# The down projections of a two-FFN block: 16 turns of at most three pairs in place of 14 of at most four, with another order of the seven products

## The chip, the cores and the metric

The kernel runs on one core of a Trainium2 chip. The metric is device microseconds of one execution. The profile is of one execution of its own, with its own time; the other times are of runs without a profile.

## The reference

One layer over a sequence of 1024 positions and 1024 features, in float32: x = x + ½·SwiGLU₁(norm(x)); then a mixer (eight heads of stick-breaking attention beside a gated short convolution) that adds to x; then x = x + ½·SwiGLU₂(norm(x)); a last norm. What matters here are the two FFNs:

```
def swiglu(h, w_gate, w_up, w_down):
    return (jax.nn.silu(h @ w_gate) * (h @ w_up)) @ w_down
```

w_gate and w_up are 1024 × 2816, w_down is 2816 × 1024. The change touches the two products with w_down, called the down phases.

## The kernel before, in words

**Arithmetic.** Every float32 operand of a matmul is split in two parts, a rounded one (`hi`, written by ACT, line 169) and the rest (`lo`, written by DVE, line 170), and three matmuls make one product (`mm3`, line 221). On top of that the FFNs use a 2 × 2 block scheme with seven products in place of eight, P1, P2, P3, P5, P6, P7 and Q4. Each product has a left factor (the stationary operand) and a right factor (the moving one), which are sums and differences of the four blocks. Two products can share a PSUM bank (`BANK`, line 562): P1 and P2 have bank 0, P6 bank 1, P7 and Q4 bank 2, P5 and P3 bank 3. The first of two that share has to be taken out of PSUM before the second may be added on top of it.

**A down phase.** The 2816 hidden features are 22 tiles of 128, or 11 pairs; `NQ` is 11. The output is cut into four groups g; a group is the output tiles g and g + 4, in two halves of 512. So there are 44 units (a pair for a group), each of seven products of three matmuls of 128 × 128 by 128 × 512, or 21 matmuls. A **turn** (`Turn`, line 782) runs one group over some consecutive pairs q0 to q1, product by product. `UPTO` and `TURNS` (lines 374 and 375) list the turns: here 14, over 2, 3, 4, 4, 3, 3, 3, 4, 4, 4, 4, 3, 2 and 1 pairs. The first ten end before the last pair: ACT and DVE take their products out of PSUM (lines 802 to 829), and each sends four accumulating DMAs, which add 256 KB to memory each (line 795, issued by POOL: 40 in a phase). The last four turns, one per group, add into tiles that were read back (`back`) and call `ready` four times (lines 831 to 855). In the first down phase `ready` is `to_mixer` (line 963: split with the gain, squares for the next norm, a store); in the second it is `to_output` (line 1326: squares, the final norm, the store of the result).

**Factors.** The left factors of a turn are made during the turn before it, one step after each product. In the first phase they come from w_down (`left`, line 463; raw tiles in two buffers, loaded by `L.load`), in the second from memory (`left_back`, line 500, which loads seven factors and splits them). The right factors of a pair are made once and kept in SBUF until the last turn that needs them: in the first phase from memory (`right_back`, line 723, which has one load under way ahead of the split), in the second from w_down (`right_rows`, line 738). `down_prep` (line 770) steps the left and the right generators of a turn side by side. The seven products run in the order `FEW`: P1, P6, P2, P7, P5, Q4, P3.

**Buffers.** Tiles of 128 × 512 (`s`, line 58) have 72 buffers, those of 128 × 1024 (`w4`, line 62) ten. The left factors of one turn take six of the ten (three pairs of hi and lo; the seventh factor is in `s` tiles), and raw or intermediate tiles take more.

**Order.** The framework puts the instructions of each engine in one queue, nearly in the order in which the program states them, and each engine runs its queue in order; matmuls of neighbouring products may be mixed. All plain loads are on SP's queue in order, all accumulating DMAs on POOL's. An instruction that waits for a buffer or for data holds up all behind it on its engine.

After the first down phase comes the V projection (line 981), which takes the features in the order of `VORDER` (line 435): tiles 2 and 6, then 3 and 7, 0 and 4, 1 and 5. After the second one nothing follows but the stores.

## Time and profile before

| | us |
|---|---|
| median of three runs | 1953.84 (1951.84 to 1957.67) |
| the profiled execution: its time | 1946.61 |
| the profiled execution: its span | 1944.9 |
| mean granted clock of TensorE, of full speed | 0.977 |

A row of windows gives a stretch: its length, then the busy time of each engine with its number of instructions, the granted clock of TensorE, the share of the 16 DMA engines and GB/s. A row of waits tells who waited for whom: microseconds in total, times, the longest. A row of groups has the shape, the number of instructions, busy time and the mean ns of one, then the idle time of the engine before them. PE is TensorE, DVE is VectorE, ACT is ScalarE, POOL is GpSimd, SP is SyncE.

### The profile page before, as it was taken

The numbers are of one execution on the slowest core, as the hardware profiler recorded it, in microseconds if no ns is written. First come the engines' busy times: TensorE is split into PE (matmuls) and PEld (weight loads), VectorE is DVE, ScalarE is ACT, GpSimd is POOL, SyncE is SP. The second block draws the span as 40 slices with busy tenths as digits, with TensorE's granted clock in tenths as the row PEclk, the third lists the DMA queues.
The fourth block names the chain that finished last, engine by engine and source line by source line (L and its number), as shares of the span: only waits on it lengthen the run. The fifth ranks groups of instructions, "written<-read, shape, count | busy, mean of one in ns | idle before, by whom it ended". The sixth has DMA issues, their size and how long they took to land. (4 is left out here: it accounts for less than half of the span.)

```text
span 1944.9 us, 23049 instructions
## 1 busy us (share of the span) xinstructions
PE 1845.2 (95%) x8176; PEld 1506.7 (77%) x8176; DVE 1384.8 (71%) x2145; ACT 887.6 (46%) x1576; POOL 238.2 (12%) x384
## 2 busy tenths in 40 slices
PE   6889999999898989999999999989999999889996
PEld 5668888888677768888888877867888888667784
DVE  4897666666766698577787898668666666657667
ACT  4543222233544446567687785533322222345443
POOL 1101101000121111110101000200101001012111
PEclk8899999999999999999999999999999999989998
DMA  7114333324787843432313333313333333488864
GB/s 233 65 55 135 106 104 111 103 93 143 203 214 194 220 154 101 95 77 60 96 37 78 97 107 117 129 38 103 114 109 104 108 101 109 147 209 190 214 166 153
DMA packets 250277, 242.73 MB, mean 125 GB/s; under 512 B 13568, under 2 KB 196400, under 8 KB 250160
## 3 DMA queue, kind: packets, MB, share of 16 engines
q1 hardware_dynamic: 216720, 157.87, 26.8%
q0 software_dynamic: 33440, 83.38, 16.6%
q8 instruction: 64, 1.05, 0.2%
q14 instruction: 53, 0.43, 0.1%
HBM read 150.76 MB, written 81.00 MB: 119 GB/s over the span
## 5 line engine op out<-in xcount | busy, mean ns | idle before, releaser
L91 PE MATMUL ps<-s,w 128*128 128x512 f32 x6352 | 1533.2, 395 | 72.0 <-ACT s L169 19.7
L91 PEld LDWEIGHTS ps<-s,w 128*128 128x128 f32 x6352 | 1192.6, 190 | 339.4 <-ACT s L169 24.5
L169 ACT CAST w<-raw 128x1024 fp32r<-128x1024 f32 (+3 forms) x154 | 156.9, 1019 | 271.5 <-PE ps L91 167.8
L170 DVE TENSOR_TENSOR w<-raw,w 128x1024 fp32r<-128x1024 f32 (+3 forms) x154 | 181.6, 1180 | 110.9 <-PE ps L91 61.3
L91 PE MATMUL ps<-s,s 128*128 128x512 f32 (+3 forms) x968 | 246.6, 382 | 14.0 <-DVE s L835 8.5
L91 PEld LDWEIGHTS ps<-s,s 128*128 128x128 f32 x968 | 181.7, 189 | 55.9 <-ACT s L818 6.7
L634 POOL DMA_DIRECT2D c_sp<-s x154 | 83.5, 542 | 782.4 <-DVE s L620 618.7
L170 DVE TENSOR_TENSOR w<-w,w 128x1024 fp32r<-128x1024 f32 (+3 forms) x96 | 104.6, 1090 | 95.4 <-PE ps L91 48.6
L170 DVE TENSOR_TENSOR s<-s,s 128x512 fp32r<-128x512 f32 (+2 forms) x190 | 125.7, 676 | 58.0 <-ACT s L169 56.9
L169 ACT CAST s<-s 128x512 fp32r<-128x512 f32 (+2 forms) x190 | 111.4, 611 | 73.5 <-DMA s<-c_sp 45.9
L169 ACT CAST w<-w 128x1024 fp32r<-128x1024 f32 (+3 forms) x96 | 90.1, 938 | 98.4 <-DMA w<-c_sp 86.6
L616 ACT ACTIVATE s<-s 128x512 f32<-128x512 f32 x40 | 25.3, 633 | 209.1 <-DVE s L615 209.1
L484 DVE TENSOR_TENSOR w<-raw 128x1024 f32<-128x1024 f32 (+3 forms) x54 | 62.9, 1164 | 56.0 <-PE ps L91 55.9
L170 DVE TENSOR_TENSOR s<-raw,s 128x512 fp32r<-128x512 f32 (+2 forms) x120 | 78.5, 672 | 13.0 <-ACT s L169 12.7
L601 ACT ACTIVATE s<-ps 128x512 f32<-128x512 f32 x40 | 23.8, 598 | 122.8 <-PE ps L91 122.8
L169 ACT CAST s<-raw 128x512 fp32r<-128x512 f32 (+2 forms) x120 | 70.7, 607 | 8.1 <-DMA raw<-in_ffn_w_down 8.1
L1204 DVE TENSOR_TENSOR s<-s,ps 128x128 f32<-128x128 f32 (+2 forms) x96 | 52.7, 549 | 16.8 <-ACT s L1200 16.4
L1192 ACT ACTIVATE s<-ps 128x128 f32<-128x128 f32 (+2 forms) x96 | 47.0, 490 | 37.7 <-PE ps L91 37.3
L607 DVE TENSOR_TENSOR s<-s,ps 128x512 f32<-128x512 f32 x40 | 27.4, 686 | 47.8 <-PE ps L91 47.8
L1200 ACT ACTIVATE s<-s 128x128 f32<-128x128 f32 (+2 forms) x96 | 50.2, 523 | 20.9 <-DVE s L1196 19.7
L637 DVE TENSOR_TENSOR s<-s,s 128x512 f32<-128x512 f32 x88 | 56.8, 687 | 1.3
L620 DVE SCALAR_TENSOR_TENSOR s<-s,s 128x512 f32<-128x512 f32 x80 | 54.8, 687 | 1.9 <-ACT s L616 0.7
(135 smaller groups left out, 1639.1 us busy)
## 6 DMA issues: line engine op xcount, KB each, us to landing
c_sp<-s POOLq DMA_DIRECT2D x154, 256.0 KB, 2.5
raw<-in_ffn_w_gate SPq DMA_DIRECT2D x43, 512.0 KB, 3.9
raw<-in_ffn_w_up SPq DMA_DIRECT2D x43, 512.0 KB, 5.2
s<-c_sp SPq DMA_DIRECT2D x83, 256.0 KB, 6.4
x_sp<-s POOLq DMA_DIRECT2D x72, 256.0 KB, 4.1
r_sp<-s POOLq DMA_DIRECT2D x56, 256.0 KB, 4.5
raw<-in_ffn_w_down SPq DMA_DIRECT2D x11, 1024.0 KB, 7.7
raw<-in_w_in SPq DMA_DIRECT2D x20, 512.0 KB, 3.8
```

The lines of the kernel that those rows point to most:

```text
L91: nc.tensor.matmul(out, lhs, rhs, **kw)
L169: nc.scalar.copy(hi, x)
L170: nc.vector.tensor_tensor(out=lo, in0=x, in1=f(hi), op=ALU.subtract)
L484: nc.vector.tensor_tensor(out=two(y), in0=two(blk(1, 2)), in1=blk(3).unsqueeze(1).to_broadcast([P, 2, n]), op=ALU.add)
L607: nc.vector.tensor_tensor(out=self.u3, in0=self.u2, in1=self.o[2], op=ALU.add)
L616: last_silu[0] = nc.scalar.activation(self.u2, self.u2, AF.Silu)
L620: nc.vector.scalar_tensor_tensor(out=u, in0=u, scalar=-0.5, in1=g, op0=ALU.mult, op1=ALU.mult)
L634: nc.gpsimd.dma_start(out=self.sp[FACTORS.index(self.names[i]), j], in_=x)
L637: nc.vector.tensor_tensor(out=out, in0=x, in1=y, op=op)
L1192: behind(nc.scalar.activation(u["s"][:, cols], u["z"][:, cols], AF.Exp), table_set)
L1200: nc.scalar.activation(sc, sc, AF.Ln, bias=1.0)
L1204: nc.vector.tensor_tensor(out=sc, in0=sc, in1=u["z"][:, cols], op=ALU.max)
```

## The change

The turns get other lengths: 16 turns over 2, then twelve of 3, then 2, 2 and 2 pairs (the thirteenth, the first of the last four, has 3). Their products run in a new order, P1, P7, P5, P6, P2, Q4, P3. The right factors are no longer tied to a turn: a list `MADE` says how many of the 77 are made by the end of each turn, and they are made one after the other. In the first phase four loads are under way ahead of the split. The left factors are made in the order P2/P1, P7/P5, P3/P6, Q4; in the second phase each load of them stands one step ahead of its split. In the last turns of the groups the order of the additions differs. The gate and up part keeps its order. `VORDER` stays.

```diff
@@ -371,12 +371,9 @@
     c_sp = [dr.tile([7, NQ, P, HALF], F32, name=f"c_sp{i}") for i in range(2)]
 
 
-    UPTO = (2, 3, 4, 4, 5, 6, 7, 8, 9, 10) + (NQ,) * 4
+    UPTO = (2, 3, 3, 3, 5, 6, 6, 6, 8, 9, 9, 9) + (NQ,) * 4
+    MADE = (21, 22, 25, 35, 42, 43, 46, 56, 63, 64, 67) + (7 * NQ,) * 5
     TURNS = [(i % 4, UPTO[i - 4] if i > 3 else 0, n) for i, n in enumerate(UPTO)]
-
-    def news(i):
-
-        return range(UPTO[i - 1] if i else 0, UPTO[i])
 
     def part(c0, src, **kw):
 
@@ -393,14 +390,14 @@
             yield [part(j * S, w[:, m * P : (m + 1) * P]) for j, w in enumerate((wg, wu))]
         for j, (g, q0, q1) in enumerate(TURNS):
             if i:
-                for q in news(j):
-                    yield [part(0, wd[2 * q * P : 2 * (q + 1) * P])]
                 continue
             n = (q1 - q0) * P
             rows = wd[2 * q0 * P : 2 * q1 * P].rearrange("(k two p) c -> two p k c", two=2, p=P)
             yield [(b * n, n, (lambda a: a.rearrange("p (k c) -> p k c", c=P)),
                     rows[two, :, :, d * P : (d + 1) * P])
                    for b, (two, d) in enumerate(((1, g), (0, g), (1, g + 4), (0, g + 4)))]
+        for q in range(NQ * i):
+            yield [part(0, wd[2 * q * P : 2 * (q + 1) * P])]
 
     def mixer_weights():
         def columns(c0):
@@ -460,7 +457,8 @@
 
 
 
-    def left(raw, n=HALF):
+    def left(raw, n=HALF, late="P7"):
+
 
         a = {}
 
@@ -486,13 +484,18 @@
         nc.vector.tensor_tensor(out=blk(3), in0=y[:, :n], in1=blk(2), op=ALU.add)
         nc.vector.tensor_tensor(out=blk(0), in0=blk(3), in1=blk(0), op=ALU.add)
         yield
-        z = two(raw[:, : 4 * n])[:, 0::3]
-        hi, lo = pair(), pair()
-        split(two(hi), two(lo), z)
-        halves(hi, lo, "P3", "P6")
-        yield
-        halves(*split(pair(), pair(), y), "P7", "P5")
-        yield
+
+        def wide():
+            hi, lo = pair(), pair()
+            split(two(hi), two(lo), two(raw[:, : 4 * n])[:, 0::3])
+            halves(hi, lo, "P3", "P6")
+
+        def narrow():
+            halves(*split(pair(), pair(), y), "P7", "P5")
+
+        for step in (wide, narrow) if late == "P7" else (narrow, wide):
+            step()
+            yield
         a["Q4"] = split(s(F32R)[:, :n], s(F32R)[:, :n], blk(2))
         L.load()
         yield
@@ -506,17 +509,26 @@
             nc.sync.dma_start(out=to.rearrange("p (k c) -> p k c", c=P),
                               in_=c_sp[1][i, q0:q1, :, g * P : (g + 1) * P].rearrange("k p c -> p k c"))
 
-        yield a
-        for i in (0, 2, 4):
+        def begin(i):
             raw = w4(F32)[:, : 2 * n]
             for j in range(2):
                 load(raw[:, j * n : (j + 1) * n], i + j)
-            parts = split(w4()[:, : 2 * n], w4()[:, : 2 * n], raw)
+            return raw
+
+        yield a
+        raw = begin(0)
+        yield
+        for i, after_it in ((0, 4), (4, 2), (2, 6)):
+            now = raw
+            if after_it < 6:
+                raw = begin(after_it)
+            else:
+                raw = s()[:, :n]
+                load(raw, 6)
+            parts = split(w4()[:, : 2 * n], w4()[:, : 2 * n], now)
             for j in range(2):
                 a[FACTORS[i + j]] = tuple(x[:, j * n : (j + 1) * n] for x in parts)
             yield
-        raw = s()[:, :n]
-        load(raw, 6)
         a["Q4"] = split(s(F32R)[:, :n], s(F32R)[:, :n], raw)
         yield
 
@@ -712,72 +724,95 @@
                 prep = left(L.take()[0])
                 a = next(prep)
             else:
-                prep = down_prep(i, 0)
-            for name in FEW:
+                prep = iter(())
+                makers[i] = Prep(i)
+                makers[i].begin(0)
+            for n, name in enumerate(FEW):
                 unit.do(name)
                 next(prep, None)
+                if i in makers:
+                    makers[i].step()
+                    makers[i].upto(UPTO[0] * (n + 1))
             run(prep)
+        makers[i].end()
 
     ring, lefts = {}, {}
 
-    def right_back(q):
-
-        b = ring[q] = {}
-
-        def load(name):
-            raw = s()
-            nc.sync.dma_start(out=raw, in_=c_sp[0][FACTORS.index(name), q])
-            return raw
-
-        raw = load(FEW[0])
-        for i, name in enumerate(FEW):
-            now, raw = raw, load(FEW[i + 1]) if i < 6 else None
-            b[name] = split(s(F32R), s(F32R), now)
+    ORDER = ("P1", "P7", "P5", "P6", "P2", "Q4", "P3")
+
+    def rights_back(ahead=4):
+
+        todo = [(q, name) for q in range(NQ) for name in ORDER]
+        raws = []
+
+        def load():
+            q, name = todo[len(raws)]
+            raws.append(s())
+            nc.sync.dma_start(out=raws[-1], in_=c_sp[0][FACTORS.index(name), q])
+
+        for i, (q, name) in enumerate(todo):
+            while len(raws) < min(len(todo), i + ahead):
+                load()
+            ring.setdefault(q, {})[name] = split(s(F32R), s(F32R), raws[i])
             yield
 
-    def right_rows(q):
-
-        b = ring[q] = {}
-        raw, _ = L.take()
-        b11, b12, b21, b22 = (raw[:, i * HALF : (i + 1) * HALF] for i in range(4))
+    def rights_rows():
+
+
+        def done(name, x):
+            b[name] = split(s(F32R), s(F32R), x)
 
         def comb(out, x, y, op):
             nc.vector.tensor_tensor(out=out, in0=x, in1=y, op=op)
             return out
 
-        def done(name, x):
-            b[name] = split(s(F32R), s(F32R), x)
-
...
+        for q in range(NQ):
+            b = ring[q] = {}
+            raw, _ = L.take()
+            b11, b12, b21, b22 = (raw[:, i * HALF : (i + 1) * HALF] for i in range(4))
+            done("P1", b11)
+            comb(b11, b11, b12, ALU.subtract)
             yield
+            done("P7", comb(b12, b22, b12, ALU.subtract))
+            yield
+            done("P5", b11)
+            yield
+            done("P6", comb(b11, b11, b22, ALU.add))
+            yield
+            done("P2", b21)
+            comb(b21, b11, b21, ALU.subtract)
+            yield
+            done("Q4", b21)
+            yield
+            done("P3", b22)
+            L.load()
+            yield
+
+    class Prep:
+
+
+        def __init__(self, i):
+            self.i, self.made, self.lefts = i, 0, iter(())
+            self.rights = rights_rows() if i else rights_back()
+
+        def upto(self, n):
+            while self.made < n:
+                next(self.rights)
+                self.made += 1
+
+        def begin(self, j):
+            if j < len(TURNS):
+                g, q0, q1 = TURNS[j]
+                self.lefts = left_back(g, q0, q1) if self.i else left(L.take()[0], (q1 - q0) * P, "P3")
+                lefts[j] = next(self.lefts)
+
+        def step(self):
+            next(self.lefts, None)
+
+        def end(self):
+            run(self.lefts)
+
+    makers = {}
 
     class Turn(Blocks):
 
@@ -836,17 +871,15 @@
 
             if name == "P6":
                 u = self.kept.pop(self.g)
+                comb(x(1, 1), u, ALU.subtract)
+                ready(self.g + 4, 1)
+                comb(x(1, 0), u, ALU.subtract)
                 comb(x(0, 1), u, ALU.add)
-                comb(x(1, 1), u, ALU.subtract)
-                comb(x(1, 0), u, ALU.subtract)
             if name == "P2":
                 comb(x(0, 0), o, ALU.add)
                 ready(self.g, 0)
-            if name == "P7":
+            if name in ("P7", "P5"):
                 comb(x(1, 1), o, ALU.subtract)
-            if name == "P5":
-                comb(x(1, 1), o, ALU.subtract)
-                ready(self.g + 4, 1)
             if name == "Q4":
                 comb(x(1, 0), o, ALU.subtract)
                 ready(self.g + 4, 0)
@@ -856,17 +889,21 @@
 
     def down(i, acc, tiles, back, ready):
 
-        for j, (g, q0, q1) in enumerate(TURNS):
-            prep = down_prep(i, j + 1) if j + 1 < len(TURNS) else iter(())
-            if j + 1 >= NQ - 1 and j + 1 < len(TURNS):
+        prep = makers.pop(i)
+        for j in range(len(TURNS)):
+            k = j + 1
+            prep.begin(k)
+            if len(TURNS) - 4 <= k < len(TURNS):
                 for hf in range(2):
-                    back((j + 1) % 4, hf)
-                    back((j + 1) % 4 + 4, hf)
+                    back(k % 4, hf)
+                    back(k % 4 + 4, hf)
             turn = Turn(j, acc, tiles)
-            for name in FEW:
+            made = MADE[j - 1] if j else 7 * UPTO[0]
+            for n, name in enumerate(ORDER):
                 turn.do(name, ready)
-                next(prep, None)
-            run(prep)
+                prep.step()
+                prep.upto(made + (MADE[j] - made) * (n + 1) // 7)
+            prep.end()
         ring.clear()
         lefts.clear()
 
```

## Rows read from the trace of the kernel before

**Rows 1.** The page's first line.
```profile
span 1944.9 us, 23049 instructions
```

**Rows 2.** Windows: first down phase (two rows), V stage, second down phase (four), end.
```profile
core 0: us, PE busy (x) PEld busy (x) DVE busy (x) ACT busy (x) POOL busy (x), PEclk, DMA share, GB/s
494.00:671.00 177.00, 162.46 (x691) 129.23 (x690) 114.94 (x159) 87.53 (x146) 35.36 (x42) 0.99 0.79 200
671.00:728.00 57.00, 48.41 (x203) 38.33 (x202) 50.73 (x86) 24.38 (x41) 8.50 (x15) 0.94 0.52 165
728.00:752.00 24.00, 24.00 (x108) 19.57 (x107) 15.93 (x31) 15.29 (x33) 5.35 (x10) 0.94 0.38 131
1689.00:1876.00 187.00, 168.82 (x694) 132.60 (x693) 120.27 (x172) 90.05 (x148) 36.15 (x43) 0.95 0.85 207
1876.00:1895.00 19.00, 19.00 (x85) 15.73 (x85) 11.83 (x20) 6.02 (x12) 1.67 (x2) 1.00 0.57 151
1876.00:1936.00 60.00, 51.78 (x210) 39.93 (x209) 43.96 (x86) 20.85 (x48) 6.31 (x7) 0.94 0.51 155
1936.00:1945.00 9.00, 0.20 (x1) 0.00 (x0) 3.23 (x8) 2.57 (x6) 1.85 (x2) 0.50 0.31 117
```

**Rows 3.** Waits, 494 to 671 us: who waited for whom, total, times, longest.
```profile
ACT s L169 <- DMA s<-c_sp: 38.5, 12, 8.9
PE ps L91 <- ACT s L818: 4.6, 3, 2.6
PE ps L91 <- ACT s L169: 3.4, 1, 3.4
```

**Rows 4.** Waits, 1689 to 1876 us.
```profile
ACT w L169 <- DMA w<-c_sp: 59.1, 21, 6.2
ACT s L169 <- DMA raw<-in_ffn_w_down: 8.1, 1, 8.1
PE ps L91 <- ACT s L169: 6.5, 3, 4.1
PE ps L91 <- DVE s L820: 5.2, 5, 1.8
```

**Rows 5.** Waits of SP's queue: first phase, then second.
```profile
SPq L191 <- DVE s L170: 125.3, 13, 13.1
...
SPq L506 <- PE ps L91: 130.2, 30, 8.3
```

**Rows 6.** Windows of 5 us, columns as in rows 2.
```profile
605.00:610.00 5.00, 5.00 (x16) 3.95 (x17) 5.00 (x8) 2.68 (x6) 1.73 (x2) 0.70 0.41 57
1700.00:1705.00 5.00, 3.29 (x6) 1.57 (x6) 3.37 (x5) 1.24 (x2) 0.00 (x0) 0.52 1.05 319
1805.00:1810.00 5.00, 5.00 (x24) 4.14 (x23) 3.74 (x5) 2.45 (x6) 1.59 (x2) 1.00 1.11 328
```

**Rows 7.** DMA queues and issues: 494 to 671 us, then 1689 to 1876.
```profile
q0 software_dynamic: 5816, 11.07, 37.0%
s<-c_sp SPq DMA_DIRECT2D x57, 256.0 KB, 7.5
...
q0 software_dynamic: 5835, 11.23, 37.5%
w<-c_sp SPq DMA_DIRECT2D x36, 256.0 KB, 5.2
w<-c_sp SPq DMA_DIRECT2D x22, 192.0 KB, 3.7
```

**Rows 8.** Groups by line, 494 to 671 us: what takes products out of PSUM.
```profile
L795 POOL DMA_DIRECT2D x_sp<-s x39 | 33.8, 869 | 140.3 <-ACT s L814 77.4 <-DVE s L820 20.8 <-ACT s L828 18.0
L820 DVE TENSOR_TENSOR s<-s,ps 128x512 f32<-128x512 f32 x10 | 6.8, 680 | 0.2 <-ACT s L818 0.2
L814 ACT COPY s<-ps 128x512 f32<-128x512 f32 x10 | 5.8, 579 | 3.2 <-PE ps L91 3.2
```

**Rows 9.** Timeline of the last turn: start, us, engine, line, operation, idle before it.
```profile
1923.52 0.41 ACT L169 CAST w<-w 128x256 fp32r<-128x256 f32 x1 [5.68 <-DMA w<-c_sp]
...
1928.74 2.80 PE L91 MATMUL ps<-s,w 128*128 128x512 f32 x6 [3.34 <-ACT w L169]
...
1936.24 0.69 DVE L835 TENSOR_TENSOR s<-s,ps 128x512 f32<-128x512 f32 x1
```

27 lines of the change are left out of this document (removed).

## The prediction, made before the change was run

> **What bounds the kernel now.** I read the page's first line, then windows over both down phases, then the waits inside them, then queues and groups. The span is 1944.9 us [rows 1]; the profiled execution's own time is 1946.61, so 1.7 lie around the span. The median of the three runs is 1953.84, 0.37% higher; the sum is made against 1946.6 and carried to the median by that ratio. The change touches only the two down phases, so only their idle time is at stake.
>
> I cut each phase at its last four turns. The cut comes after 34 of the 44 units: the first phase is 177.0 us for 34 units and 57.0 for ten, the second 187.0 and 60.0, and 9.0 after the last product [rows 2]. The clean rate comes from 1876 to 1895: TensorE is busy for all of 19.00 us at full clock, and this is the turn of four pairs, 84 matmuls (the row counts 85, one being cut by the window's edge). So a matmul costs 0.227 us and a unit of 21 matmuls 4.77 us. 34 units are 162 us clean, ten are 47.7. What is lost now: 15 and 25 us in the long stretches, 9 and 12 us in the last turns. 44 units stay 44 units, so the matmuls' own time cannot change; the four losses can.
>
> Why the long stretches lose: in the first phase ACT stands 38.5 us before casts of right factors, until their loads land, 8.9 at the longest [rows 3]. ACT's queue is in order, so the copy of P7 out of PSUM (line 818), behind such a cast, comes late and TensorE waits for it, 4.6 us, and 3.4 for a cast itself [rows 3]. The loads are late because SP's queue is in order too: the next raw w_down load (line 191) waits 13 times, up to 13.1 us, for DVE to free its buffer, and the single load ahead of the right factors is behind it [rows 5]. In the second phase it is the left factors: ACT waits 59.1 us for them [rows 4], since their 30 loads wait for TensorE to give back one of the ten wide buffers, 130 us on SP's queue [rows 5]; TensorE then waits for line 820, behind them on DVE, in five turns [rows 4]. A single wait of 8.1 us for w_down [rows 4] is the start of the second phase: pair 2 is requested only when pair 0's buffer is free, and pairs 0 and 1 were made side by side. A long idle stretch also costs clock: after 603 us the granted clock is 0.70 of full, after 1700 it is 0.52 [rows 6], which is the lower level, 1.2 GHz, for most of these stretches.
>
> **The change, part by part.**
>
> *Order of the products.* Bank 0 is used again three products later instead of one (P1, then P7, P5, P6, then P2), bank 2 three instead of one, bank 3 three instead of one. With three pairs a product is 9 × 0.227 = 2.0 us, so an eviction has 6 us in place of 2 (2.7 with four pairs). A late copy behind a cast, the 4.6 us of rows 3 and the 5.2 of rows 4, is covered unless it is over 6 us late. The order also frees the wide buffers as they are needed: P7/P5 go free after the third product, P2/P1 after the fifth, and the new left factors are made in an order that fits into ten. So DVE no longer stands before a `lo` part until a product has run.
>
> *Loads ahead.* Right factors: four of the 77 under way. On average 4.8 factors are made per turn of 14.3 us, one in 3.0 us, so a load has some 12 us; landing takes 7.5 [rows 7]. In the three turns that make ten (the fourth, eighth and twelfth) it is 1.4 us each, 5.7 us of cover, which is too little: I leave 2 us of stall each, 6 per phase. SP's 13.1 us behind line 191 remain.
>
> *Shorter turns.* Two more turns that end outside the last pair, so per phase eight more accumulating DMAs, eight copies on ACT and six operations on DVE: 8 × 0.58 = 4.6 us of ACT, 6 × 0.68 = 4.1 us of DVE and 8 × 0.87 = 7.0 us of POOL's issue [rows 8]. ACT is busy 87.5 of 177 us, DVE 114.9 [rows 2]: they hide beside the matmuls; with the cover gone they would cost the sum of the first two, 8.7 us. In the ten-factor turns DVE has no room: 7 operations for the left factors, 10 for the right ones and 3 out of PSUM are 20, at the stretch's mean (114.94/159 = 0.72) 14.5 us in a turn of 14.3; in the second phase 4, 16 (11 for each pair's seven factors) and 3 are 23, at 120.27/172 = 0.70, 16 us [rows 2].
>
> *The DMA engines* are the dearest term. The queue of the accumulating DMAs holds 37.0% of 16 engines over 177 us for 39 of them, so one is 1.68 us of all sixteen (1.80 in the second phase) [rows 7]. Eight more are 13.4 and 14.4 us. The long stretch of now has a DMA share of 0.79 and 0.85 [rows 2], that is 140 and 159 us of DMA time; with the one unit more that it will hold, and the eight, 156 and 176. The clean time of 35 units is 167. The first fits; the second is over it. Single windows run at 1.05 and 1.11 [rows 6], so a share of 1.0 over a long stretch is not excluded, but loads land later. Bounds for the second phase: 167 (all hidden) to 176/0.85 = 207 (the present share is the most there is). I take 178, near the share of 1.0, since windows beyond it exist.
>
> The Trainium skill's page "DMA: Bandwidth & Descriptors" (section "Measured") wants DMAs of 1 MiB and gives about 2.0 us per DMA plus its bytes over 436 GB/s; by that, loads of 192 KB in place of 256 are a loss, and the 14 more left loads in the second phase would be 28 us if each were waited for (an estimate from that page). Here the 192 KB loads land in 3.7 us, those of 256 KB in 5.2 [rows 7], so the smaller ones are not held up by a fixed part of that size, and they run beside each other.
>
> *First long stretch:* 167 + 6 = 173 against 177: −4. *Second:* 178 against 187: −9; most of it is the start of the phase, where pair 2 is now requested after half a unit instead of a whole one, about 9 us earlier than now.
>
> *Last four turns.* Now 4, 3, 2, 1 pairs, then 3, 2, 2, 2: nine units, 42.9 us clean instead of 47.7. DVE does the same additions, and the left factors made beside them are of six pairs in both. It is busy 50.7 of the 57 us in the first phase [rows 2], so it is the bound there. First product and these 50.7: 2 + 51 = 53, against 57: −4. After it the V stage takes tiles 3 and 7, now the last turn's, second and not first to third: cover of 24 matmuls, 5.4 us, where it was three times that. That stretch is full now (24.00 of 24.00) [rows 2]. Between 0 and 5 us, I take +1. In the second phase DVE is busy 43.96 + 3.23 = 47 of 69 us [rows 2]; 2 + 47 + the 6 of the last row in which DVE is idle (9.0 − 3.23) are 55, TensorE's floor is 42.9 + 8.7 (the time from the last addition at 1936.24 to the end, rows 9) = 52. Now it takes 69: the turn of one pair has nothing to hide its left load, 5.68 us of ACT and 3.34 of TensorE [rows 9]. Turns of two hide some of it. I leave 8 us of waits: 62, −7.
>
> Sum: −4 − 9 − 4 + 1 − 7 = −23, 1946.6 → 1923.6, and 1930 against the median.
>
> **The rivals.** *All stalls go* (DMA runs beyond 1.0): long stretches 169 each, ends at 53 and 55, the V stage as it was: −8 − 18 − 4 − 14 = −44, 1910. For it: windows above 1.0; against it: the ten-factor turns and the SP queue. Chance 0.13.
>
> *Given back*: in each ten-factor turn DVE is over the turn by 0.2 to 1.6 us and a load by 1.8 (7.5 − 5.7), so TensorE waits another 3 us, six times, +18: −5, about 1949. For it the count of DVE; against it that a late factor is needed late in the next turn. Chance 0.12.
>
> *The clock falls in the last turns* (slower). With DVE setting the pace, TensorE has 28.6 us of work in the three turns of two pairs and idles about half as long; if that idling comes in one piece per turn, the lower level returns each time. At 1.2 GHz a matmul is 0.45 us, 42 are 19 us, three turns 57, and with 14.3 for the first 71.5: +14.5 in the first phase, and 80 against 69, +11, in the second. With −13 from the long stretches and +1 that is +13.5, 1967. It decides from about half of those turns at the lower level, where the sum is zero. For it: the last turn of each phase is half idle now, and its stretches have a mean clock of 0.94 [rows 2]; against: the fall after 603 came behind 3.4 us of idling at a stretch [rows 3, 6], and the three-product distance cuts waits short. The Trainium skill's "TensorE: Matmul & The Clock Gate" (section "HAM oscillation") says that bursts with waits between them can throttle again in every round. The trace has such falls [rows 6], but no row here has one repeated turn by turn. Chance 0.12.
>
> *The DMA engines are the bound* (slower): the shares 0.79 and 0.85 are what these streams sustain. Then 156/0.79 = 197 and 176/0.85 = 207: +20 + 20 − 10 at the ends, 1977, or 1984 at the median. Against it are the windows above 1.0 [rows 6]; for it that both phases have such a mean. The page on DMA above ends on this side too; what its rule would do here, a fixed part waited out for each load, would leave ACT's 59.1 us for left factors standing [rows 4], and I count it into this case. Chance 0.08.
>
> **How the numbers follow.** My forecast has 0.55. A measurement of this kernel tells about 0.3%, 6 us, from no change. Faster by more: 0.55 + 0.13 + half of the third case = 0.73 (rounded down); within: 0.07; slower: the clock and the DMA case, 0.20. The range from 1907 to 1960 leaves out half of the best case, half of the clock case and all of the DMA case, 0.20.
>
> **What would show it.** Right: ACT's waits for c_sp in the long stretches fall from 38.5 and 59.1 us to under half; no wait of TensorE for lines 818 and 820; the start of the second phase without its 8 us wait; a DMA share of 0.9 or more in the second stretch; DVE near 90% in the last four turns of the first phase. Wrong: a granted clock of 0.5 in several of the last turns, or TensorE waiting for casts of right factors throughout a phase at a DMA share that has not risen.

## The result, and the profile after

The changed kernel takes 1923.11 us (median of four runs, 1917.72 to 1924.48), the kernel before 1955.07 beside it: a ratio of 0.983, with an interval of 0.981 to 0.986. The profiled execution took 1924.48. The forecast was 1930, in a range from 1907 to 1960. The total came out near the forecast; its parts did not, so the nearness is luck.

The page's first line:

```profile
span 1922.8 us, 23200 instructions
```

Windows of the changed kernel. The first two rows are the two stretches that most comparisons below use. Each begins where ACT starts the last SiLU of a P2 product (line 613, in the last gate/up unit); the first ends at the first exponential of the attention (line 1229), so it holds the first down phase and the V projection, and the second ends with the span. The others answer to [rows 2], cut after 35 units, as the turns now end: long stretch, last four turns, V stage; long stretch, last four turns, end.

```profile
473.60:781.80 308.20, 296.72 (x1298) 243.71 (x1297) 231.91 (x359) 163.35 (x282) 67.63 (x94) 0.99 0.74 192
1655.10:1922.80 267.70, 235.09 (x967) 187.29 (x965) 184.38 (x299) 125.09 (x230) 51.51 (x61) 0.94 0.78 193
...
486.00:653.00 167.00, 167.00 (x738) 138.26 (x737) 121.20 (x183) 94.13 (x162) 42.01 (x50) 1.00 0.95 231
653.00:707.00 54.00, 44.33 (x183) 34.61 (x181) 51.85 (x89) 27.53 (x47) 9.91 (x17) 0.97 0.59 186
707.00:731.00 24.00, 22.19 (x99) 18.42 (x99) 17.97 (x32) 13.87 (x30) 6.37 (x9) 0.93 0.38 121
1670.00:1862.00 192.00, 172.50 (x719) 138.09 (x719) 119.42 (x176) 89.45 (x154) 41.20 (x49) 0.96 0.87 203
1862.00:1915.00 53.00, 47.81 (x186) 37.28 (x184) 48.90 (x96) 25.75 (x58) 7.99 (x9) 0.90 0.61 181
1915.00:1923.00 8.00, 0.00 (x1) 0.00 (x0) 3.00 (x7) 2.17 (x4) 1.79 (x2) 0.65 0.35 131
```

The same two stretches of the kernel before:

```profile
475.90:800.60 324.70, 301.17 (x1291) 241.79 (x1290) 228.27 (x340) 158.12 (x266) 59.15 (x86) 0.98 0.65 176
1675.30:1944.90 269.60, 234.50 (x963) 183.81 (x962) 178.81 (x283) 119.97 (x214) 44.85 (x53) 0.94 0.72 185
```

The first stretch is 16.5 us shorter, the second 1.9. Of the first, 12.0 are idle time of TensorE (length less PE busy: 23.5 before, 11.5 now) and 4.5 are TensorE's busy time (301.17 before, 296.72 now, at a granted clock of 0.98 and 0.99). The second has nearly its old idle time (35.1 before, 32.6 now) and its old clock, 0.94. The span is 22.1 us shorter; the 3.7 us that are in neither stretch are not followed here. So three quarters of the gain lie in the first phase, whose long stretch now has no wait at all: 167.00 of 167.00 us busy, with the DMA engines at 0.95.

Waits of the changed kernel, who waited for whom, first long stretch (486 to 653 us), to be held against [rows 3]:

```profile
ACT s L169 <- DMA s<-c_sp: 17.3, 12, 3.4
```

And the second (1670 to 1862 us), against [rows 4]:

```profile
ACT w L169 <- DMA w<-c_sp: 39.9, 11, 10.4
...
PE ps L91 <- ACT w L169: 7.7, 2, 6.1
...
PE ps L91 <- ACT s L853: 6.5, 4, 3.6
...
PE ps L91 <- DVE s L840: 3.5, 1, 3.5
```

ACT's waits for right factors fell from 38.5 to 17.3 us, and no wait of TensorE came of them. Its waits for left factors are fewer (11 against 21) but longer, up to 10.4, and TensorE still waits behind them. SP's queue in the second long stretch, to be held against [rows 5]:

```profile
SPq L509 <- DVE w L170: 34.1, 16, 3.6
SPq L509 <- DMA w<-c_sp: 33.1, 11, 8.7
SPq L509 <- PE ps L91: 32.1, 10, 7.1
SPq L191 <- DVE s L170: 29.0, 7, 7.8
```

Where TensorE's longest waits of that stretch lie (timeline, TensorE: start, us, operation, the idle time before it):

```profile
1707.68 2.93 PE L91 MATMUL ps<-s,w 128*128 128x512 f32 x6 [6.14 <-ACT w L169]
...
1775.56 3.78 PE L91 MATMUL ps<-s,s 128*128 128x512 f32 x8 [3.60 <-ACT s L853]
...
1838.92 2.50 PE L91 MATMUL ps<-s,w 128*128 128x512 f32 x5 [3.52 <-DVE s L840]
```

By the number of matmuls run up to there, these are the third, the seventh and the eleventh turn. Each stands just ahead of a turn in which ten right factors are made, and makes three itself. That is the pattern that the experiments followed up.

How far one profiled execution can be trusted: the first stretch has the same program in five of the kernels here and took 308.2, 308.0, 308.4, 307.9 and 311.5 us, the second has it in two and took 267.7 and 263.4 (with the old turns, in two others, 247.5 and 247.7). So differences of up to 4 us between single stretches are left alone below.

### The profile page after: what moved, and what is told of

Read it like the earlier page. It is cut to its first block, busy times and chain, and to the rows that moved or that the text cites. A ratio compares the mean times of both kernels' runs of the same rounds, so it can differ in the third digit from the quotient of the medians.

```text
span 1922.8 us, 23200 instructions
## 1 busy us (share of the span) xinstructions
PE 1835.9 (95%) x8176; PEld 1507.5 (78%) x8176; DVE 1393.1 (72%) x2179; ACT 897.9 (47%) x1608; POOL 253.5 (13%) x400
## 4 chain that ended last, share of the span: by engine, by line
PE 69%; issue 15%; DVE 9%; DMA 3%; POOL 3%; ACT 1%; SPq 1%; POOLq 0%; DVEq 0%; ACTq 0%
PE ps L91 68%; DVE w L170 1%; DVE s L870 1%; POOL r_sp L830 1%; DMA w<-c_sp 1%; POOL c_sp L646 1%; DVE s L170 1%; DMA raw<-in_ffn_w_gate 1%; DVE s L269 1%; DVE s L176 1%; PE ps L277 0%; DVE s L700 0%; DMA s<-x_sp 0%; PE ps L1087 0%; DVE s L544 0%
## 5 line engine op out<-in xcount | busy, mean ns | idle before, releaser
L169 ACT CAST w<-raw 128x1024 fp32r<-128x1024 f32 (+2 forms) x158 | 157.5, 998 | 278.6 <-PE ps L91 187.9
L170 DVE TENSOR_TENSOR w<-raw,w 128x1024 fp32r<-128x1024 f32 (+2 forms) x158 | 182.0, 1153 | 117.6 <-PE ps L91 60.2
L646 POOL DMA_DIRECT2D c_sp<-s x154 | 83.5, 542 | 777.7 <-DVE s L632 610.9
L170 DVE TENSOR_TENSOR w<-w,w 128x768 fp32r<-128x768 f32 (+2 forms) x104 | 105.8, 1017 | 84.8 <-PE ps L91 44.3
L169 ACT CAST w<-w 128x768 fp32r<-128x768 f32 (+2 forms) x104 | 91.7, 881 | 92.5 <-DMA w<-c_sp 41.6
L170 DVE TENSOR_TENSOR s<-raw,s 128x512 fp32r<-128x512 f32 (+2 forms) x133 | 87.7, 667 | 24.2 <-ACT s L169 23.8
L169 ACT CAST s<-raw 128x512 fp32r<-128x512 f32 (+2 forms) x133 | 77.9, 602 | 36.4 <-DVE raw L766 36.4
L482 DVE TENSOR_TENSOR w<-raw 128x1024 f32<-128x1024 f32 (+2 forms) x56 | 63.1, 1128 | 43.4 <-PE ps L91 43.4
L613 ACT ACTIVATE s<-ps 128x512 f32<-128x512 f32 x40 | 23.8, 598 | 122.8 <-PE ps L91 122.8
L1241 DVE TENSOR_TENSOR s<-s,ps 128x128 f32<-128x128 f32 (+2 forms) x96 | 52.6, 548 | 16.8 <-ACT s L1237 16.4
L830 POOL DMA_DIRECT2D r_sp<-s x48 | 41.6, 876 | 154.7 <-DVE s L855 50.5
L830 POOL DMA_DIRECT2D x_sp<-s x48 | 41.6, 866 | 125.4 <-DVE s L855 57.7
```

Of the source, the lines that this page charges most:

```text
L169: nc.scalar.copy(hi, x)
L170: nc.vector.tensor_tensor(out=lo, in0=x, in1=f(hi), op=ALU.subtract)
L482: nc.vector.tensor_tensor(out=two(y), in0=two(blk(1, 2)), in1=blk(3).unsqueeze(1).to_broadcast([P, 2, n]), op=ALU.add)
L613: last_silu[0] = nc.scalar.activation(self.s0, o, AF.Silu)
L646: nc.gpsimd.dma_start(out=self.sp[FACTORS.index(self.names[i]), j], in_=x)
L830: nc.gpsimd.dma_start(out=self.acc(self.g + 4 * i, hf), in_=x, accum_op=ALU.add)
```

## The experiments

In the table the first column of stretches is the first down phase with the V projection, the second the second down phase to the end of the span. Each ratio is to runs of the kernel before taken beside it, whose medians lie between 1951.94 and 1955.07.

| kernel | median, us | ratio to before (95%) | first | second |
|---|---|---|---|---|
| before | 1955.07 | 1 | 324.7 | 269.6 |
| the change | 1923.11 | 0.983 (0.981 to 0.986) | 308.2 | 267.7 |
| change, one load ahead of right factors | 1959.98 | 1.004 (1.003 to 1.006) | 348.8 | 263.4 |
| change, old order of products | 1940.54 | 0.993 (0.991 to 0.996) | 311.5 | 283.0 |
| change, old turns | 1906.56 | 0.977 (0.974 to 0.979) | 309.3 | 247.5 |
| change, old turns and old order | 1915.15 | 0.980 (0.978 to 0.983) | 311.8 | 255.3 |
| change, right factors made evenly | 1907.28 | 0.977 (0.975 to 0.979) | 309.4 | 247.7 |
| change, eight additions left out | 1922.26 | 0.985 (0.983 to 0.987) | 311.5 | 263.4 |
| change, nine loads of w_down left out | 1906.34 | 0.976 (0.973 to 0.979) | 307.9 | 246.2 |
| change, raw left factors in small tiles | 1932.80 | 0.989 (0.987 to 0.992) | 308.0 | 274.0 |
| the same, two steps ahead | 1938.30 | 0.994 (0.992 to 0.996) | 308.4 | 277.1 |
| even factors, twelve wide buffers | 1918.94 | 0.982 (0.980 to 0.985) | 315.3 | 259.0 |
| old turns, other VORDER | 1905.30 | 0.977 (0.975 to 0.979) | 309.9 | 247.7 |
| even factors, two additions on GpSimd | 1905.39 | 0.975 (0.972 to 0.978) | 307.8 | 252.9 |

### What brings the first phase its gain

One load ahead instead of three. (`ahead=4` has four loads under way, the one that is being split among them, so three stand ahead of it.)

```
-    def rights_back(ahead=4):
+    def rights_back(ahead=2):
```

> The changed kernel with one part undone: in the first down phase the right factors have, as before, one load under way ahead of the split instead of three. The stretch from the last gate/up unit to the first exponential of the attention (first down phase and V projection) takes 324.7 us before the change and 308.2 after it. Theory A (the loads ahead bring the first phase's gain): ACT's waits for these loads go back from 17.3 to some 38 us between 486 and 650 us, the stretch goes to about 320, the kernel to about 1935. Theory B (the greater distance between products that share a bank brings it, since a late copy out of PSUM then has 6 us instead of 2): ACT's waits rise just the same, but TensorE does not feel them, the stretch stays at 311 or less and the kernel within 3 us of 1923. Either way the second phase stays at 267.6.

The kernel became slower than the one before, and all of it lies in the first stretch. Its windows row:

```profile
475.90:824.70 348.80, 313.43 (x1293) 250.03 (x1292) 231.72 (x359) 162.22 (x282) 67.61 (x94) 0.94 0.66 170
```

Its waits from 490 to 670 us:

```profile
ACT s L169 <- DMA s<-c_sp: 40.9, 11, 7.2
...
PE ps L91 <- ACT s L853: 13.3, 4, 4.7
PE ps L91 <- ACT s L837: 6.3, 1, 6.3
```

ACT's waits came back (40.9 us), and the copies of P7 and P1 out of PSUM (lines 853 and 837) came late behind them, so that TensorE waited up to 6.3 us for one in spite of the three products between two uses of a bank. Theory A holds and B falls, and the effect is larger than A said: 348.8, not 320. Part of that is the clock: the same matmuls took 313.43 us instead of 296.72, 16.7 us more, at 0.94 of the clock instead of 0.99, on top of 24 more of idle time. Without the loads ahead the change is worse in this stretch than the kernel before (348.8 against 324.7). That the bunches of ten factors are the reason is likely but not shown: the even list of factors was not run with one load ahead.

### Order of the products and length of the turns

The old order, the old turns, and both. Of the old order only the loop is shown; the left factors and the last additions go back to the order that goes with it, while the right factors are still made in the new one.

```
-            for n, name in enumerate(ORDER):
+            for n, name in enumerate(FEW):
```
```
-    UPTO = (2, 3, 3, 3, 5, 6, 6, 6, 8, 9, 9, 9) + (NQ,) * 4
-    MADE = (21, 22, 25, 35, 42, 43, 46, 56, 63, 64, 67) + (7 * NQ,) * 5
+    UPTO = (2, 3, 4, 4, 5, 6, 7, 8, 9, 10) + (NQ,) * 4
+    MADE = tuple(7 * n for n in UPTO[1:]) + (7 * NQ,)
```

> The changed kernel with the seven products of the down phases in the old order (and the left factors and the last additions in the order that goes with it); turns of three and four loads ahead stay. Theory A (the loads ahead bring the first phase's gain): the stretch of the first phase with the V projection stays within 3 us of 308.2. Theory B (the distance brings it): TensorE again waits for lines like 818 and 820, and the stretch goes back to 318 or more. Second phase (267.6 from the last gate/up unit to the end): if the order helps to free the wide buffers, it grows by 5 or more; if its loads are held up by these buffers in either order, it stays within 3. Kernel: 1923 to 1926 by A, 1935 or more by B.

> The changed kernel with the turns of before (14 turns over 2, 3, 4, 4, 3, 3, 3, 4, 4, 4, 4, 3, 2 and 1 pairs, the right factors made turn by turn to match); the new order of products and the loads ahead stay. Theory: the turn length alone brings little in the long stretches, since the work is the same; the first phase with V stays within 4 us of 308.2 and the second phase loses up to 5 by its last turn of one pair (3.3 us of waiting there before): 1923 to 1932. Rival: the turns of three bring the gain, because the left factors of a turn are then smaller and the right factors are spread evenly: the first phase goes back to 318 or more and the kernel to 1935 or more. Second rival: the eight accumulating DMAs saved per phase matter more: the second phase gets shorter than 267.6 by 5.

> The changed kernel with both the turns of before and the old order of products (as in the run with the old order): of the change there remain the right factors made as one list with four loads ahead and pair 2 asked for early, and the left loads one step ahead. Stretches so far: first phase with V 324.7 before, 308.2 changed; second phase 269.6 before, 267.6 changed, 247.5 with the turns of before and the new order, 283.0 with turns of three and the old order. Theory G (the new order matters only where factors come late, and the loads ahead carry the rest): first phase 309 to 313, second 247 to 253, kernel 1905 to 1913. Rival H (the order, by the greater distance between products that share a bank, is what the second phase gains by): second phase 260 or more, kernel 1918 or more, with TensorE waiting for copies out of PSUM.

The first stretch hardly minds any of it: 311.5, 309.3 and 311.8, as theory A (loads ahead) had it. The second minds both. With the old order it is 283.0, and TensorE waits for P7's copy again; waits of that kernel from 1670 to 1945 us:

```profile
PE ps L91 <- ACT s L853: 14.8, 4, 7.9
PE ps L91 <- DVE s L870: 4.7, 1, 4.7
...
PE ps L91 <- ACT s L837: 4.1, 2, 3.9
```

So in the second phase the order is worth 15.3 us beside the turns of three and 7.8 beside those of four (255.3 less 247.5), between theory G, which gave it at most some 5 us there, and H, which gave it 12 or more.

The surprise is the old turns: 1906.56, 16.6 us under the change, all of it in the second stretch. None of the three expectations had 20 us there; the rival in which turns of three help is the wrong way round, and 5 us were as much as eight saved additions were to give. The old turns bring two things back at once, the lengths and at most seven factors in a turn. The next runs part them.

### What the turns of three cost in the second phase

The turns of three stay, and the list of right factors is smoothed (at most seven in each of these turns):

```
-    MADE = (21, 22, 25, 35, 42, 43, 46, 56, 63, 64, 67) + (7 * NQ,) * 5
+    MADE = (21, 25, 28, 35, 42, 46, 49, 56, 63, 67, 70) + (7 * NQ,) * 5
```

> The changed kernel with the right factors made evenly in both down phases: 3 to 7 of them in each of the first twelve turns instead of 1, 3, 10 and 7 by turns. Theory F (the ten-factor turns, for which ACT and DVE have no room in 14.3 us, make the turns of three dear in the second phase): the second phase falls from 267.6 to 257 or less, the first one (308.2) by at most 2, kernel about 1912. Theory E (the left factors' chain per turn): second phase 264 or more, kernel 1920 to 1926. It can also come out slower, if the factors made earlier hold buffers that other work waits for: first phase 311 or more.

Theory F holds, by more than it said: the second stretch is 247.7, what the old turns give. Its row for the second long stretch:

```profile
1670.00:1862.00 192.00, 183.45 (x790) 149.30 (x789) 137.96 (x206) 100.66 (x175) 44.28 (x53) 0.98 0.93 220
```

SP's waits there:

```profile
SPq L509 <- PE ps L91: 65.9, 19, 9.8
SPq L509 <- DVE w L170: 35.3, 18, 3.2
...
SPq L191 <- DVE s L170: 14.6, 4, 8.9
```

In the same 192 us TensorE runs 790 matmuls instead of 719, and the DMA engines rise from 0.87 to 0.93. Counted in matmuls, 13 of the 20 us that the phase gains lie in the third, the seventh and the eleventh turn (together 63.2 us in the change, 50.0 with the even list). The length of the turns itself costs nothing that can be seen (247.7 against 247.5). SP's waits for a wide buffer are longer than in the change, 65.9 us for TensorE alone, and do no harm that can be seen.

The eight additions that the two more turns bring, left out:

```
+            self.out = not (phase and j in (5, 9))
...
-            nc.gpsimd.dma_start(out=self.acc(self.g + 4 * i, hf), in_=x, accum_op=ALU.add)
+            if self.out:
+                nc.gpsimd.dma_start(out=self.acc(self.g + 4 * i, hf), in_=x, accum_op=ALU.add)
```

> The changed kernel without the eight accumulating DMAs of its sixth and tenth turn in the second down phase, so that this phase sends as many as before the change (those additions to the output are left out). The second phase takes 267.6 us with turns of three, and 247.5 when the turns are those of before and all else is kept. Theory D (the eight more accumulating DMAs, by the queue's rows 1.8 us of all 16 engines each, make the turns of three dear): the phase falls by 10 or more, to 257 or less, kernel about 1912. Theory E (it is the chain from load to cast to split of the left factors, whose length per turn does not shrink with the turn): the phase stays at 263 or more, kernel 1918 to 1925. The first phase is the same.

Theory D falls: 1922.26 against 1923.11, with intervals that overlap. The second stretch is 4.3 us shorter, no more than two executions of one program differ by.

And the list uneven as in the change, but without nine loads of w_down:

```
-        for q in range(NQ * i):
+        for q in range(2 * i):
             yield [part(0, wd[2 * q * P : 2 * (q + 1) * P])]
...
-            raw, _ = L.take()
+            if q < 2:
+                raws.append(L.take()[0])
+            raw = raws[q % 2]
```

> The changed kernel, with its uneven list of right factors, without nine of the eleven loads of w_down in the second phase: the two raw tiles are loaded once and combined again and again (this leaves out loading the other nine pairs, so the right factors are those of other data); all work of ACT, DVE and TensorE stays. The even list took the second phase from 267.6 to 247.7 us. Theory J (two megabytes of w_down asked for in the turns of ten factors, none in the two turns before, crowd the left factors' loads): with the transfers gone the uneven list costs little, second phase 252 or less. Theory K (the burst is in the work of ACT and DVE: casts of ten factors stand in their queues before the left factors): the phase stays at 260 or more. Between 252 and 260 both have a part.

The size is J's: 246.2 us, with all the work of DVE and ACT as uneven as it was, so K falls: the uneven work is not enough by itself. Row of the second long stretch:

```profile
1670.00:1862.00 192.00, 185.00 (x801) 150.42 (x799) 138.71 (x211) 101.61 (x178) 45.21 (x54) 0.99 0.84 179
```

So the uneven list costs where w_down has to be loaded as well. How much of these 21 us any kernel would gain by nine loads of 1 MiB less stays open: the even list was not run without them. And J's picture of it, two loads at once in the turns of ten factors, is not what the traces show. SP's timeline between 1720 and 1800 us, w_down loads (line 191) and groups of left loads (line 509), first of the changed kernel:

```profile
1727.09 0.40 SPq L191 DMA_DIRECT2D raw<-in_ffn_w_down  x1
...
1728.14 15.23 SPq L509 DMA_DIRECT2D w<-c_sp  x9
1743.46 0.45 SPq L191 DMA_DIRECT2D raw<-in_ffn_w_down  x1
...
1758.06 0.37 SPq L191 DMA_DIRECT2D raw<-in_ffn_w_down  x1
1758.53 18.40 SPq L509 DMA_DIRECT2D w<-c_sp  x6
```

The same of the kernel with the even list:

```profile
1722.61 0.51 SPq L191 DMA_DIRECT2D raw<-in_ffn_w_down  x1
...
1738.37 0.37 SPq L191 DMA_DIRECT2D raw<-in_ffn_w_down  x1
...
1753.31 0.37 SPq L191 DMA_DIRECT2D raw<-in_ffn_w_down  x1
...
1756.50 12.98 SPq L509 DMA_DIRECT2D w<-c_sp  x6
```

The loads go out one by one in both, some 15 us apart. What differs is when. A pair's buffer is free, and the next load goes out, only when the seventh factor of that pair is made: by the matmuls that TensorE has run, these requests stand at 10.4, 13.8 and 16.4 units in the change and at 9.1, 12.4 and 15.6 with the even list. For the first of them the list itself is the reason, which places that factor in the fourth turn and not in the third; the second stands behind nine left loads (line 509) that held SP for 15.2 us; only before the third does SP wait for DVE, 6.6 us.

The third request is the one that hurts, since the left factors of the next turn are requested right behind it, 0.5 us later and not 3.2 as with the even list. Issues of the changed kernel, the four left loads between 1758 and 1762 us, then all of the second long stretch (KB each, median us from issue to landing):

```profile
w<-c_sp SPq DMA_DIRECT2D x4, 192.0 KB, 13.2
...
w<-c_sp SPq DMA_DIRECT2D x67, 192.0 KB, 5.6
```

What comes of it, from ACT's timeline of the changed kernel:

```profile
1763.19 0.62 ACT L169 CAST s<-raw 128x512 fp32r<-128x512 f32 x1
1774.18 0.83 ACT L169 CAST w<-w 128x768 fp32r<-128x768 f32 x1 [10.37 <-DMA w<-c_sp]
1774.92 0.59 ACT L853 ACTIVATE s<-ps 128x512 f32<-128x512 f32 x1
```

ACT stands 10.4 us before the cast of a left factor, the copy of P7 (line 853) is next in its queue, and TensorE waits 3.6 us for it at 1775.56. The other two long waits of TensorE, at 1707.68 and 1838.92, have the same thing ahead of them. SP's timeline before each:

```profile
1692.41 0.37 SPq L191 DMA_DIRECT2D raw<-in_ffn_w_down  x1
1693.41 17.83 SPq L509 DMA_DIRECT2D w<-c_sp  x8
...
1823.06 0.37 SPq L191 DMA_DIRECT2D raw<-in_ffn_w_down  x1
1823.48 14.98 SPq L509 DMA_DIRECT2D w<-c_sp  x6
```

Here ACT stands 6.2 and 8.9 us before the cast of a left factor. Taking the w_down loads away can have helped in two ways: no 1 MiB transfer beside the left factors' own, or no request of w_down that waits on SP's queue for DVE with theirs behind it (29.0 us of such waits in the change, 14.6 with the even list). The 13.2 us to landing speak for the first, but SP had also stood 7.8, 6.6 and 2.7 us before these three w_down requests, and no run tells the two apart.

### What I had held responsible: the wide buffers and the chain of the left factors

Raw left factors in tiles of 128 × 512, one step and then two steps ahead:

```
-        def begin(i):
-            raw = w4(F32)[:, : 2 * n]
+        def begin(*names):
+            raws = []
+            for i in names:
+                raws.append(s()[:, :n])
...
+        raws = begin(0, 1)
```
```
...
+        raws = [begin(0, 1), begin(4, 5)]
```

> The changed kernel with one thing different in the second down phase: the raw left factors are loaded one by one into tiles of 128 x 512 (72 buffers) and not two by two into the ten wide ones, and split one by one. Theory C (the second phase stays stalled because these loads wait for a wide buffer): the waits of SP for wide buffers at the left loads, 44.5 us for TensorE and 40.0 for DVE in the changed kernel, vanish; ACT's waits for left factors fall from 39.9 to under 15 us; the second phase goes from 267.6 to 260 or less, the kernel to about 1915. Rival D (the eight more accumulating DMAs hold up the loads): loads are requested earlier and land later, ACT's waits stay over 30 us and the phase within 3 us of 267.6. The price on the way: six casts and six subtractions in place of three and three of twice the size, some 3 us of ACT and of DVE per turn at most.

> The changed kernel with the raw left factors of the second phase in tiles of 128 x 512, as in the run before with that change (second phase 274.0), but requested two steps ahead of their split instead of one. Theory E (the left factors' chain of load, cast and split, with one load step under way, is longer than a turn of three pairs): ACT's waits for these loads fall from 56.2 to under 25 us, and the second phase to 258 or less, kernel 1914 or less. Theory D or F (transfers, or the factors of the ten-factor turns): ACT's waits stay above 40 us and the phase within 4 of 274. The price on the way is as in that run, some 3 us of ACT and of DVE per turn at most.

Both are slower than the change, 274.0 and 277.1 us in the second stretch. SP's queue in the first of the two, 1670 to 1862 us:

```profile
SPq L191 <- DVE s L170: 78.7, 8, 12.4
...
SPq L509 <- PE ps L91: 13.2, 14, 3.4
```

ACT's wait for the left factors in the same stretch:

```profile
ACT w L169 <- DMA s<-c_sp: 56.2, 14, 9.7
```

The waits for a wide buffer nearly vanish, as theory C said, and nothing is won: SP, no longer held there, comes sooner to the next w_down load and stands there, 78.7 us in place of 29.0, with the left loads behind it in the queue. ACT's waits rise to 56.2. In the kernel with two steps ahead it is 83.5 and 60.4. Theories C and E fall. Splitting one by one adds some 4 us of work to ACT and to DVE in the whole stretch, which is not what these waits are.

Twelve wide buffers on the even list:

```
-        return sb.tile([P, HALF], dt, name=nm("s"), tag="s", bufs=72)
+        return sb.tile([P, HALF], dt, name=nm("s"), tag="s", bufs=68)
...
-        return sb.tile([P, S], dt, name=nm("w"), tag="w", bufs=10)
+        return sb.tile([P, S], dt, name=nm("w"), tag="w", bufs=12)
```

> The version with evenly made right factors (1907.3; second phase 247.7, in which SP waits 65.9 us for TensorE to free a wide buffer) with twelve wide buffers in place of ten, and 68 tiles of 128 x 512 in place of 72. Theory (the wide buffers still set when left factors are asked for): SP's waits at the left loads fall by half, the waits of TensorE at 1688 and 1709 us (2.4 and 3.0 us) go, second phase 243 or less, kernel about 1902. Rival: that request comes early enough as it is, and the lost tiles of 128 x 512 cost: second phase 247 or more, or the first phase above 311.

The rival, and worse: 315.3 and 259.0. SP's waits for TensorE at the left loads went from 65.9 to 4.5 us, those for DVE from 35.3 to 76.2: again one wait in place of another, and ACT's waits for left factors went from 23.8 to 44.3. In the first phase the lost tiles of 128 × 512 show: ACT and DVE stand 10.9 us before tiles that accumulating DMAs still read, 2.5 with ten wide buffers. The run changes both numbers of buffers, so what the second phase lost is not tied to either.

### The last turns

VORDER in the order in which the last turns end (on the kernel with the old turns), and two of P6's additions given to GpSimd (on the even list):

```
-    VORDER = ((2, 6), (3, 7), (0, 4), (1, 5))
+    VORDER = ((0, 4), (1, 5), (2, 6), (3, 7))
```
```
...
-                comb(x(1, 0), u, ALU.subtract)
-                comb(x(0, 1), u, ALU.add)
+                comb(x(1, 0), u, ALU.subtract, nc.gpsimd)
+                comb(x(0, 1), u, ALU.add, nc.gpsimd)
```

> The version with the turns of before (1906.6) and VORDER put in the order in which the last turns now end: tiles 0 and 4 first, 2 and 6 and then 3 and 7 last. In that version TensorE waits 6.0 us in the V projection (at 710 us, for the split of a tile of the last turn that lies in DVE's queue) and 2.9 before it. Theory: with the last turn's tiles taken last, the 6.0 us go, and the kernel takes about 1901. Rival: DVE is the bound over the last turns, so that the same wait comes at the end of the V projection, or the attention starts no earlier: 1905 to 1908.

> The version with evenly made right factors (1907.3) with two of the three additions of P6's accumulated part in the last turns of both phases given to GpSimd, which is idle there; DVE, busy 11 to 13 of the 12 to 14 us of each last turn, has 1.36 us less to do in each. Theory (DVE is the bound of the last turns): each phase ends up to 4 us earlier, TensorE's waits for line 840 (3.2 us in the first phase, 2.6 in the second) go, kernel 1900 to 1904. Rival: GpSimd takes longer over them than DVE, and the next addition to the same tile waits for it, or they slow each other: no gain, 1906 or more.

Neither moves the time by more than the intervals: 1905.30 beside 1906.56, 1905.39 beside 1907.28. (The 252.9 us of the second are of the slowest of its four executions, 1910.58.) In the first, the wait in the V projection stays: 5.9 us at 708, for the split of a weight tile on DVE (line 170), so it is not the order of the tiles. In the second, one addition takes 1.64 us on GpSimd, where DVE needs 0.68, and TensorE's wait for line 840 near the end stays at 2.6 us.

## Why the prediction was right, and where it was wrong

The sum was −23 us on the profiled execution, the measured one −22.1. It was made of −7 for the first phase (with V) and −16 for the second; the stretches say −16.5 and −1.9, and the rest lies outside them. The forecasts for the two phases were off by some 10 and 14 us, in opposite directions, and cancelled: that the total was met is luck, though what was to bring the first phase its gain was seen rightly. Point by point:

- **The cut.** The start at 494 was read off the first copy out of PSUM, which runs late: counted in matmuls from the last gate/up unit, 1.7 units of the phase were done by then, and 1.0 at 1689. So the rows hold some 33 units each and not 34; 691 and 694 matmuls at 0.227 us are 157 and 158 us, and what was lost is 20 and 29 us, not 15 and 25. Lost time is what is compared here.
- **First long stretch**, said 173 us, "2 us of stall each" in the three ten-factor turns: 167, no stall. The step that failed is the cover of 5.7 us for a load that takes 7.5. (With three loads ahead it is even less, 3 × 1.4 = 4.3 us.) It treated a load as if TensorE needed its factor at once; ACT does wait (17.3 us in all, 3.4 at the longest), and the distance to the product that uses the factor takes it up.
- **Loads ahead** as the cure of the late casts: right, and shown by undoing it.
- **Distance of the products**: right in its mechanism, as the second phase shows (15.3 or 7.8 us); for the first phase not needed once the loads come in time.
- **Second long stretch**, said 178, 11 us of it lost: its row has 192 us with 719 matmuls, which are 163 us at 0.227, so 29 are lost, as many as before. The early request of pair 2 worked, the 8.1 us wait for w_down is gone; but waits of 1.6 and 6.1 us for left factors stand near that place, and those of the seventh and eleventh turn are new. The step that failed is "most of it is the start of the phase" with the DMA engines' share of 1.0 as the only limit: what a bunch of ten factors does to the w_down request, and what that load does to the left loads requested behind it, was not in the sum. With the even list the whole second stretch is 247.7 us, 20 below the change and 22 below the kernel before, where the forecast had 16.
- **The rival "given back"** (0.12) had the right place, the ten-factor turns, and the wrong mechanism and size. It charged DVE's 20 to 23 operations, 3 us in each of six turns. In the first phase these turns cost nothing, in the second about 20 us, most of it in the turns ahead of them, and not where nine loads of w_down are left out.
- **"The order also frees the wide buffers as they are needed"**: SP still waits for them (66 us for TensorE and DVE in the second long stretch), but it is not what costs. With longer waits of that kind (even list) the stretch is fast, and with hardly any (small tiles) it is slow.
- **DMA engines, "the dearest term"**: eight additions less, 14.4 us of engine time by the forecast, changed the time by nothing that the runs can tell. The rival that shares of 0.79 and 0.85 are all there is falls by the 0.95 of the first long stretch.
- **Last four turns**: 54 us against 53 said, DVE 51.85 of them busy, as said; in the second phase 53 and 8 against 62. Right.
- **V stage**, said +1, with up to 5: TensorE stands 4.4 us before it goes on with the V projection at 708.8 (1.8 of them in the row from 707), and the clock is 0.93, so the upper bound was nearer. The reason was another: it waits for the split of a weight tile, queued on DVE behind the last additions, and not for the tiles of the last turn.
- **The clock falling in the last turns**: it fell, to 0.90 in the last four of the second phase (0.88 and 0.79 in two of the three short turns, 1.00 in the third), but nowhere near half in each; the rival falls. (By its own figures its sum is zero at about two thirds of those turns, not at half.)

What was to show the forecast right thus holds for the first phase (waits under half, no TensorE wait for lines 853 and 855, DVE at 96% in the last four turns) and, but for the wait at its start, fails for the second (39.9 us of 59.1 left, TensorE waiting 6.5 us for line 853, share 0.87, not 0.9).

The version that beats both is the change with the even list, or with the old turns: 1907.28 and 1906.56, 0.977 of the time before, some 16 us under the change.

## What to carry to other kernels

A list that makes ten factors here and one there does not have to fail where it makes ten: what came late here were the small loads requested right behind a large one, whose own request had been put off. So follow each turn's requests through the issuing queue, not only the mean load of the engines. When a wait is removed on an in-order queue, ask which request the queue then stops at, for what stands behind it is as late as before. And where two changes share a schedule, undo each alone: here the order and the loads ahead were worth more than the whole, and the third part, the uneven list that came with the shorter turns, gave 20 us back in the second phase.

## What the hardware showed that was not expected

A mean DMA share of 0.95 over 167 us went with no idle time of TensorE at all, where 0.79 had gone with 15 us of it: here the mean share told nothing of lateness.

The same program did not always get the same clock. The end of the first phase, 690 to 720 us, first in the change, then in the kernel with eight additions left out, which is the same program up to there:

```profile
690.00:720.00 30.00, 20.68 (x82) 15.83 (x81) 25.63 (x46) 17.67 (x34) 9.90 (x16) 0.89 0.46 153
```
```profile
690.00:720.00 30.00, 21.62 (x70) 16.52 (x69) 25.09 (x43) 14.81 (x24) 9.90 (x16) 0.72 0.41 141
```

With 0.9 us less idle time TensorE ran 70 matmuls instead of 82, at 0.72 of the clock and not 0.89, after the same wait of 3.23 us for line 840 (842 in the second kernel). So this first stretch is 311.5 against 308.2 us, although its idle time is 10.9 against 11.5. The kernel with the even list has such a row too (69 matmuls, 0.72). Why the lower level held longer there no run tells; it is a reason to leave differences of this size alone.
